# PEER layer on one core: signs of listed chunks tied to their chunk, dense part of U up to chunk 88, earlier use of the dense tiles for gathered U rows

## The chip, the cores and the metric

The kernel runs on one core of one Trainium2 chip. The metric is the device time of one execution in microseconds (us). The kernel before has a median of 1894.81 us in 3 runs (1887.17 to 1896.88). Engines are named as in the profile: PE (TensorE), PEld (its weight load), ACT (ScalarE), DVE (VectorE), POOL (GpSimd), SP (SyncE, here only a queue that starts DMAs).

## The reference

One decoder layer over 256 tokens of width 2048: attention of two kinds, attention into a memory, then PEER, a retrieval of single-neuron experts, and a last rmsnorm. The change touches PEER alone:

```python
q = (xt @ w_pq).reshape(T, PEER_HEADS, 2, PEER_D_KEY // 2)
s = jnp.einsum('thpd,hpkd->thpk', q, sub_keys)
top_s, top_i = lax.top_k(s, K)
...
best_s, best_c = lax.top_k(cand.reshape(T, PEER_HEADS, K * K), K)
expert = ia * PEER_N_KEYS + ib
gate = jax.nn.softmax(best_s, axis=-1)
...
a = jnp.einsum('td,ted->te', xb, u_tab[eb])
hidden = gb.astype(xb.dtype) * jax.nn.gelu(a)
return jnp.einsum('te,ted->td', hidden, v_tab[eb])
```

Each of 256 tokens picks 8 times 16 of 16384 experts. An expert has a row of U (2048 numbers) and a row of V.

## The kernel before

**Dense and listed chunks.** The 16384 experts are 128 chunks of 128. For chunks 0 to `C1` - 1 (83) the kernel multiplies U with all 256 tokens, whether an expert was picked or not (`u_chunk`, the "dense" chunks). For the rest, the "listed" chunks, it first finds which experts were picked by any token, writes the rows of their gates as packed lists to memory, and gathers only the U rows on these lists (`listed_products`). Experts are sorted by class: picked by one token only (`UONE`), by several tokens of one half of the sequence (`UFEW0`, `UFEW1`), or by both halves (`UALL`). `CAPS[2]` gives each class its number of tiles of 128 rows. Rows beyond a class go to `UALL`, and if that overflows as well, a slow loop (`rest`) does the remainder at the end.

**One dense chunk.** It has two halves. In each, SP loads half of the chunk's U (512 KB) into one of four `raw` tiles, ACT rounds it to `hi` (L75), DVE subtracts to get `lo` (L77; `self.last_lo` is the latest of these), and PE does 8 matmuls with `hi` (L93) and 8 with `lo` (L95). Then ACT and DVE join the two sums (L128, L129), and ACT applies gelu (L824).

**The table of gates.** The gates are scattered into a table in memory with 256 indirect writes by POOL (`put_gate`, L1170), 16 as each of 16 top-k results is finished; the kernel asks for four beside each block of work. By the counters in the code, 38 dense chunks have been emitted when the last top-k piece is out, 60 writes are then left, and `end` is 38 + 15 = 53. At chunk `end + 9` = 62 it emits the reads of the table for the listed chunks (`table_read`, L811), straight into their tiles `hb`. From chunk 63 on it takes items from `marks`: first one sign and count for each pair of listed chunks (`signs`, ACT L833 and DVE L834), up to six items a chunk, and then the seven steps that turn counts into positions (`lists`, ending in `where`, L1047). After these come 44 indirect writes (L1054) that place the listed rows, four a chunk. From chunk 65 to 82 one read a chunk fetches the gates of four dense chunks into a `raw` tile (L811, `gates`), and DVE multiplies them into the hidden values (L759).

**The listed part.** Each of 39 tiles reads its rows of gates (`lb`, L880), gathers 128 rows of U (`urows`, POOL L884), and, for class `UONE`, the matching tokens too (`xr`, POOL L895). `UONE` tiles are one DVE product (L904). The others are transposed by PE (L920), split by ACT and DVE (L921, L922) and multiplied (L93 and L95, or L937 and L940 where one half of the tokens is enough). Beside each quarter of a tile the kernel pops one step or one write of the lists of part 0 (chunks 0 to 75, 76 writes, L1054). `where` of these writes is ready at L1047 too.

**Tiles.** The dense chunks and the listed ones live in tiles of 8 chunks, 8 of them in pool `ba` (chunks 0 to 63) and 8 in pool `bb` (64 to 127). The same tiles are used again: `lb`, `urows` and `xr` of the first 14 listed tiles take theirs from `bb`, whose listed chunks are free once their rows are written; from the 15th on `urows` and `xr` come from `ba`, where a tile is free when the eight writes of part 0 that read it are done.

**Order.** Every engine works through its own queue in order. That order is not the order of the code: the framework sorts the instructions by priority along a timeline of its own (`schedule_with_timeline_sim=True`), so that an instruction whose inputs it holds to be ready can be put ahead of others that come earlier in the code. `add_manual_dep` adds a dependency that it must keep. After the listed part comes the V phase (L1249), which gathers V rows for all lists and ends with the norm and the stores.

Of the kernel before, what the change touches and what calls it, by code (L numbers as in the profile page):

```python
# [22 lines left out]
SYNC = mybir.DependencyInfo(mybir.DependencyClass.Sync, mybir.DependencyReason.DATA)  # L23
AF = mybir.ActivationFunctionType
# [15 lines left out]

C1 = 84
PARTS = ((0, 76), (76, 123), (C1, 128))
ONE0, ONE1, FEW0, FEW1, ALL = range(5)
CAPS = ((14, 14, 5, 5, 14), (10, 10, 4, 4, 10), (12, 4, 5, 18))
UONE, UFEW0, UFEW1, UALL = range(4)
UTILES = sum(CAPS[2])
assert PARTS[1][1] == C1 + UTILES
BASE, ROWS = [], []  # L50
for caps in CAPS:
    BASE.append([sum(caps[:j]) * 128 for j in range(len(caps))])
# [4 lines left out]
class Layer:  # L57
# [138 lines left out]
    def run(self):  # L196
        nc, tc, a = self.nc, self.tc, self.a
        with ExitStack() as top:
# [19 lines left out]
            self.rows = [self.dram.tile([n + (hi - lo) * 128, W], F32, name="rows%d" % part)  # L218
                         for part, (n, (lo, hi)) in enumerate(zip(ROWS, PARTS))]

# [423 lines left out]
    def peer(self):  # L644
        nc, tc, a = self.nc, self.tc, self.a
        with ExitStack() as es:
# [11 lines left out]
            def some(n):  # L658
                for _ in range(n):
                    if puts:  # L660
                        puts.pop(0)()

            with ExitStack() as e2:
# [55 lines left out]
                src = self.gw.tile([128, T], F32, tag="a", name="before_f", bufs=2)[:, :128]  # L719
# [4 lines left out]
                self.count = cl.tile([128, 2, 128], F32, name="count")  # L724
                self.rcount = self.count[:, :, C1:]
                self.over = cl.tile([128, 3], F32, name="over")
# [7 lines left out]
                marks, writes = [], []  # L734
                while c < C1:
                    if c % GROUP == 3 and first <= c + 5 < C1:
                        n = min(GROUP, C1 - c - 5)
                        self.table_read(self.buf[(c + 5) // GROUP][:, :n, :T], c + 5)
                    if c == end + 9:
                        for i in range(C1, 128, GROUP):  # L740
                            i -= i % GROUP
                            n = max(C1 - i, 0)
                            self.table_read(self.buf[i // GROUP][:, n:, :T], i + n)
                        for i in range(C1, 128, 2):
                            marks.append(lambda i=i: self.signs(self.buf[i // GROUP][:, i % GROUP:i % GROUP + 2, :T],
                                                                self.rcount[:, :, i - C1:i - C1 + 2]))
                        steps, writes = self.lists(2, ps, "sc", 2)
                        for p in range(0, len(steps), 2):
                            marks.append(lambda p=p: [f() for f in steps[p:p + 2]])
                    if c >= end + 12 and early:  # L750
                        g = early.pop(0)
                        t = self.st.tile([128, 4 * W], F32, tag="raw", name="gates", bufs=RAW)
                        t = t[:, :4 * T].rearrange("p (i t) -> p i t", t=T)
                        self.table_read(t, g)
                        done.setdefault(c + 1, []).append((g, t))
                    self.u_chunk(c, c >= first)
                    for g, t in done.pop(c, []):
                        d = self.buf[g // GROUP][:, g % GROUP:g % GROUP + 4, :T]
                        nc.vector.tensor_mul(d, d, t)  # L759
                        self.counts(g, g + 4)  # L760
                    some(4)
                    if c >= first and c % 4 == 3:
                        self.counts(c - 3, c + 1)
                    if c > end + 9:
                        if len(marks) > 4:
                            for _ in range(min(6, len(marks) - 4)):
                                marks.pop(0)()
                        elif marks:
                            marks.pop(0)()
                        else:  # L770
                            for _ in range(4):
                                if writes:
                                    writes.pop(0)()
                    c += 1
# [51 lines left out]
            nc.vector.tensor_mul(dst, dst, t)  # L826


    def signs(self, src, dst):

        n = src.shape[1]
        t = self.gw.tile([128, 2, T], BF16, tag="b", name="signs", bufs=2)[:, :n, :]
        self.nc.scalar.activation(t, src, AF.Sign)  # L833
        self.nc.vector.tensor_reduce(out=dst, in_=t.rearrange("p i (b t) -> p b i t", b=2),  # L834
                                     axis=AX.X, op=ALU.add, apply_absolute_value=True)

# [24 lines left out]
    def listed_products(self, beside):  # L861

        nc, ps, mm = self.nc, self.ps, self.nc.tensor.matmul
        v = nc.vector
        caps = CAPS[2]
        wide = sorted(((k + 0.5) / caps[c], c, k) for c in (UFEW0, UFEW1, UALL) for k in range(caps[c]))
# [8 lines left out]
        def start(n):  # L875
            cls, k = seq[n]
            if n % GROUP == 0:
                self.lbuf.append(self.bb.tile([128, GROUP, W], F32, tag="hb", name="lb", bufs=8))
            row = self.lbuf[n // GROUP][:, n % GROUP, :]
            ins = nc.sync.dma_start(row, self.listed(2, cls)[:, k, :])  # L880
            self.after(ins, 2)
            pool = self.bb if n < 14 else self.ba
            u = pool.tile([128, GROUP * W], F32, tag="hb", name="urows", bufs=8)[:, :D]
            nc.gpsimd.indirect_dma_start(  # L884
                out=u, out_offset=None, in_=self.a["Un"],
                in_offset=bass.IndirectOffsetOnAxis(ap=row[:, T:T + 1].bitcast(U32), axis=0),
                bounds_check=16383, oob_is_err=False)
            st = state[n] = {"row": row, "u": u, "cls": cls}
            if cls == UONE:
                best = self.gw.tile([128, 8], F32, tag="best", name="best", bufs=2)  # L890
                at = self.gw.tile([128, 8], U32, tag="at", name="at", bufs=2)
                v.max(out=best, in_=row[:, :T])
                v.max_index(out=at, in_max=best, in_values=row[:, :T])
                x = pool.tile([128, GROUP * W], F32, tag="hb", name="xr", bufs=8)[:, :D]
                nc.gpsimd.indirect_dma_start(  # L895
                    out=x, out_offset=None, in_=self.xrows,
                    in_offset=bass.IndirectOffsetOnAxis(ap=at[:, 0:1], axis=0),
                    bounds_check=T - 1, oob_is_err=False)
                st["x"] = x
# [60 lines left out]
        for n in range(ahead):  # L960
            start(n)
# [23 lines left out]
    def lists(self, part, pool, tag, bufs):  # L985


        nc, tc, cl = self.nc, self.tc, self.cl
        lo, hi = PARTS[part]
        n = hi - lo  # L990
        v = nc.vector
        cap, base = CAPS[part], BASE[part]
        sides = len(cap) - 1
# [185 lines left out]
    def plan(self):  # L1179

        self.seq, self.bundles, self.ends, self.sets, self.index = [], [], [], {}, {}
        self.homes = ([self.ba] * 8 + [self.bb] * 1) * 4 + ([self.ba] * 8 + [self.bb] * 8) * 4
        a, b = CAPS[:2]
        for lists in (((0, ONE0, 0, 5), (0, FEW0, 0, a[FEW0])),
# [16 lines left out]
    def after(self, ins, part):  # L1201
        assert len(self.written[part]) == PARTS[part][1] - PARTS[part][0]
        for w in self.written[part]:
            self.tc.add_manual_dep(ins.ins, w.ins.name, SYNC, reason="rows of the lists")

    def listed(self, part, cls):

        n, r = CAPS[part][cls], BASE[part][cls]
        return self.rows[part][r:r + n * 128, :].rearrange("(k p) w -> p k w", p=128)
# [197 lines left out]
    def rest(self, hidden_pair, products, out, kept):  # L1407
# [6 lines left out]
        with tc.If(count > 0):  # L1414
# [4 lines left out]
            def places(part):  # L1419
                lo, hi = PARTS[part]  # L1420
                n = hi - lo
                x = cl.tile([128, n], F32, tag="ok", name="rest_x")
                nc.vector.tensor_scalar(x, order[:, :n], self.over[:, part:part + 1], float(BIG),
                                        op0=ALU.is_ge, op1=ALU.mult)
                nc.vector.scalar_tensor_tensor(x, order[:, :n], float(ROWS[part]), x, op0=ALU.add, op1=ALU.add)
                at = cl.tile([128, n], U32, tag="where", name="rest_at")
                nc.vector.tensor_copy(at, x)
                return at
# [165 lines left out]
```

## Time and profile before

| what | value |
|---|---|
| median of 3 runs | 1894.81 us |
| the profiled execution's own time | 1893.41 us |
| its span, first to last instruction | 1891.6 us |
| mean granted PE clock in it | 0.936 |
| PE, PEld busy | 1624.2 us (86%), 1374.1 us (73%) |
| DVE, ACT, POOL busy | 1265.5 us (67%), 969.6 us (51%), 867.2 us (46%) |

A row of the windows view gives, for a stretch of the span, the busy time of PE, PEld, DVE, ACT and POOL with the number of their instructions, then the granted PE clock, the share of the DMA engines and GB/s. A row of the waits view names the waiting engine, tile and line, then what it waited for: us in total, times, the longest. A timeline row has the start, the length, the engine, the line and the operation, and in brackets the idle time before it and what ended it. The groups view has a line's instructions by shape: count, busy us, mean ns, and the idle time before them.

### The profile page before, as it was taken

To read this page: it belongs to the slowest core of one execution; us is meant where nothing else is said; L and a number is where in the kernel's file an instruction comes from. 1 tells how busy PE (TensorE), PEld (TensorE's weight loads), DVE (VectorE), ACT (ScalarE), POOL (GpSimd) and SP (SyncE) were. 2 spreads that over 40 slices of the span, in tenths; PEclk is the share of its full clock that TensorE was granted. 3 is DMA by queue.
4 is the path that set the end of the run, shared out by engine and by line. 5 is a ranking of instruction groups with operands and counts; after the bars stand their busy time and mean duration, and the time that the engine had idled before them with its cause. 6 is when DMAs were issued, how large, how long until landed. Compare 5 with 4: busy or idle time off the path is not lost. (4 is left out here: it accounts for less than half of the span.)

```text
span 1891.6 us, 25657 instructions
## 1 busy us (share of the span) xinstructions
PE 1624.2 (86%) x8790; PEld 1374.1 (73%) x8790; DVE 1265.5 (67%) x2345; ACT 969.6 (51%) x1490; POOL 867.2 (46%) x754
## 2 busy tenths in 40 slices
PE   8899999999998889999703999969448989899995
PEld 6788878878886778888603888758447877678874
DVE  6934664557688999999304559667335678677886
ACT  6434566655663446665204456444223447466765
POOL 5500001212256788888774000562777336886420
PEclk9999999999999989999956999989778999999997
DMA  7565345999655546666505667677377977998972
GB/s 273 185 229 185 127 163 171 397 391 361 194 173 188 169 130 191 200 190 190 136 1 202 210 190 265 219 261 272 124 249 292 383 298 290 373 412 321 414 313 68
DMA packets 140574, 444.38 MB, mean 235 GB/s; under 512 B 40112, under 2 KB 58230, under 8 KB 119952
## 3 DMA queue, kind: packets, MB, share of 16 engines
q1 hardware_dynamic: 91376, 217.68, 35.9%
q0 software_dynamic: 49056, 224.95, 31.0%
q8 instruction: 71, 1.16, 0.2%
q14 instruction: 71, 0.58, 0.1%
HBM read 384.12 MB, written 64.41 MB: 237 GB/s over the span
## 5 line engine op out<-in xcount | busy, mean ns | idle before, releaser
L93 PE MATMUL acc<-pair_f,hi 128*128 128x512 f32 x1872 | 496.5, 405 | 110.5 <-ACT hi L75 109.3
L77 DVE TENSOR_TENSOR lo<-raw,hi 128x1024 fp32r<-128x1024 f32 x346 | 432.2, 1253 | 206.8 <-ACT hi L75 179.7
L75 ACT ACTIVATE hi<-raw 128x1024 fp32r<-128x1024 f32 x350 | 368.4, 1057 | 317.7 <-PE acc L93 149.9
L93 PEld LDWEIGHTS acc<-pair_f,hi 128*128 128x128 f32 x1872 | 344.2, 195 | 173.3 <-ACT hi L75 111.9
L1170 POOL DMA_INDIRECT table<-total,place x256 | 327.0, 1277 | 94.7 <-issue 75.3
L95 PE MATMUL acc<-pair_f,lo 128*128 128x256 f32 x1872 | 277.3, 288 | 9.7 <-DVE lo L77 6.3
L95 PEld LDWEIGHTS acc<-pair_f,lo 128*128 128x128 f32 x1872 | 263.1, 194 | 30.7 <-DVE lo L77 8.1
L1054 POOL DMA_INDIRECT rows<-hb,where x128 | 139.6, 1091 | 48.7 <-issue 36.3
L1221 POOL DMA_INDIRECT vrows<-V,index x90 | 115.7, 1286 | 91.5 <-DVE lo L77 27.2
L86 DVE SCALAR_TENSOR_TENSOR lo<-vrows,val,hi 128x1024 fp32r<-128x1024 f32 x96 | 122.7, 1283 | 41.3 <-ACT hi L84 36.5
L84 ACT ACTIVATE hi<-vrows,val 128x1024 fp32r<-128x1024 f32 x96 | 109.1, 1147 | 70.0 <-PE out L1249 31.9
L93 PE MATMUL acc<-pair_x,hi 128*128 128x512 f32 x512 | 132.1, 396 | 0.0
L920 PE MATMUL ps_tp<-ident,urows 128*128 128x128 f32 x432 | 69.0, 295 | 63.4 <-DMA urows<-Un,lb 58.2
L77 DVE TENSOR_TENSOR lo<-vrows,hi 128x1024 fp32r<-128x1024 f32 x84 | 102.5, 1221 | 30.4 <-ACT hi L75 20.4
L834 DVE TENSOR_REDUCE count<-signs 128x4 f32<-128x512 bf16 x84 | 55.0, 677 | 100.1 <-ACT signs L833 99.2
L922 DVE TENSOR_TENSOR lo<-ps_tp,hi 128x512 fp32r<-128x512 f32 x108 | 72.7, 687 | 59.8 <-ACT hi L921 59.3
L921 ACT ACTIVATE hi<-ps_tp 128x512 fp32r<-128x512 f32 x108 | 63.3, 596 | 94.7 <-PE ps_tp L920 93.6
L920 PEld LDWEIGHTS ps_tp<-ident,urows 128*128 128x128 f32 x432 | 55.7, 152 | 71.7 <-issue 59.2
L75 ACT ACTIVATE hi<-vrows 128x1024 fp32r<-128x1024 f32 x84 | 88.2, 1053 | 36.8 <-PE out L1249 22.0
L93 PEld LDWEIGHTS acc<-pair_x,hi 128*128 128x128 f32 x512 | 91.4, 189 | 17.1 <-issue 1.4
L1249 PE MATMUL out<-hi,hh 128*128 128x512 f32 x264 | 84.3, 412 | 16.2 <-ACT hh L1256 8.1
L833 ACT ACTIVATE signs<-hb 128x512 bf16<-128x512 f32 x64 | 37.7, 622 | 111.9 <-DMA hb<-table 92.6
(423 smaller groups left out, 2820.8 us busy)
## 6 DMA issues: line engine op xcount, KB each, us to landing
raw<-U SPq DMA_DIRECT2D x168, 512.0 KB, 4.2
raw<-w_sb SPq DMA_DIRECT2D x32, 512.0 KB, 5.2
table<-zero POOLq DMA_DIRECT2D x16, 1024.0 KB, 10.7
raw<-w_out SPq DMA_DIRECT2D x32, 512.0 KB, 6.7
raw<-w_pq SPq DMA_DIRECT2D x32, 512.0 KB, 3.8
rows<-zero POOLq DMA_DIRECT2D x17, 903.0 KB, 7.2
listed<-rows SPq DMA_DIRECT2D x90, 129.0 KB, 8.5
gates<-table POOLq DMA_DIRECT2D x18, 512.0 KB, 3.8
```

The source lines that it names most:

```text
L75: nc.scalar.activation(hi, raw, AF.Copy)
L77: self.last_lo = (eng or nc.vector).tensor_tensor(out=lo, in0=raw, in1=hi.bitcast(F32), op=ALU.subtract)
L84: nc.scalar.activation(hi, raw, AF.Copy, scale=val)
L86: self.last_lo = nc.vector.scalar_tensor_tensor(lo, raw, val, hi.bitcast(F32), op0=ALU.mult, op1=ALU.subtract)
L93: mm(ps, hi[:, n * m:(n + 1) * m], pair[:, k, :], start=first and n == 0, stop=False)
L95: mm(ps[:, T:], lo[:, n * m:(n + 1) * m], pair[:, k, :T], start=False, stop=last and n == len(ks) - 1)
L920: nc.tensor.transpose(p[:, j * 128:(j + 1) * 128], st["u"][:, k * 128:(k + 1) * 128], self.ident)
L922: v.tensor_tensor(out=lo, in0=p, in1=hi.bitcast(F32), op=ALU.subtract)
L1054: ins = nc.gpsimd.indirect_dma_start(out=self.rows[part], out_offset=bass.IndirectOffsetOnAxis(ap=where[:, i - lo:i - lo + 1], axis=0), in ...
L1170: ins = self.nc.gpsimd.indirect_dma_start(out=self.table, out_offset=bass.IndirectOffsetOnAxis(ap=self.place[tb][:, s:s + 1], axis=0), in_ ...
L1221: nc.gpsimd.indirect_dma_start(out=raw, out_offset=None, in_=self.a["V"], in_offset=bass.IndirectOffsetOnAxis(ap=self.index[part, cls][:, ...
L1249: mm(out[tb][hf * 2 + q], h, v[:, q * 512:(q + 1) * 512], start=first and n == 0, stop=last and n == len(passes) - 1)
```

## The change

```diff
-C1 = 84
-PARTS = ((0, 76), (76, 123), (C1, 128))
+C1 = 88
+PARTS = ((0, 76), (76, 124), (C1, 128))
-CAPS = ((14, 14, 5, 5, 14), (10, 10, 4, 4, 10), (12, 4, 5, 18))
+CAPS = ((14, 14, 5, 5, 14), (10, 10, 4, 4, 10), (11, 4, 4, 17))
...
                             marks.append(lambda i=i: self.signs(self.buf[i // GROUP][:, i % GROUP:i % GROUP + 2, :T],
-                                                                self.rcount[:, :, i - C1:i - C1 + 2]))
+                                                                self.rcount[:, :, i - C1:i - C1 + 2], self.last_lo))
...
                         if len(marks) > 4:
-                            for _ in range(min(6, len(marks) - 4)):
+                            for _ in range(min(4, len(marks) - 4)):
                                 marks.pop(0)()
...
-    def signs(self, src, dst):
+    def signs(self, src, dst, behind=None):
...
-        self.nc.scalar.activation(t, src, AF.Sign)
+        ins = self.nc.scalar.activation(t, src, AF.Sign)
+        if behind is not None:
+            self.tc.add_manual_dep(ins.ins, behind.ins.name, SYNC, reason="not before its chunk")
...
-            pool = self.bb if n < 14 else self.ba
+            pool = self.bb if n < 11 else self.ba
```

Four things change. The sign of a pair of listed chunks now depends on the last `lo` of the dense chunk beside which it is emitted. Chunks 84 to 87 become dense, so there are 40 listed chunks and 36 listed tiles (11 `UONE`, 4 and 4 `UFEW`, 17 `UALL`; one `UONE`, one `UFEW1` and one `UALL` less), 40 writes instead of 44, 20 signs instead of 22, and part 1 of the V lists covers 48 chunk rows instead of 47. At most four marks are taken a chunk instead of six. The U rows and tokens of listed tiles 11 to 13 come from `ba` instead of `bb`.

## The prediction

> **What bounds the kernel now.** The page's slices of PE show a hole at about half of the span, so I read the waits view from 934 to 1046 us first, then the timelines of ACT, POOL and PE there, then the windows by stage.
>
> ```profile
> ACT signs L833 <- DMA hb<-table: 92.6, 3, 89.8
> PE acc L93 <- ACT hi L75: 88.1, 3, 84.1
> ...
> 934.00:1018.00 84.00, 0.19 (x2) 0.00 (x0) 1.20 (x2) 1.86 (x3) 64.17 (x67) 0.52 0.06 16
> ...
> 1046.00:1120.00 74.00, 74.00 (x425) 65.13 (x424) 36.95 (x41) 35.72 (x53) 0.00 (x0) 1.00 0.61 190
> ...
> 1212.00:1286.00 74.00, 53.28 (x242) 44.36 (x241) 41.80 (x59) 29.26 (x47) 45.89 (x45) 0.84 0.74 252
> ...
> 1336.00:1452.00 116.00, 54.64 (x342) 50.09 (x341) 40.74 (x72) 25.49 (x52) 90.37 (x84) 0.76 0.64 218
> 1452.00:1556.00 104.00, 94.46 (x631) 84.50 (x630) 73.05 (x141) 49.48 (x102) 42.42 (x40) 0.96 0.92 344
> 1556.00:1874.00 318.00, 294.62 (x1242) 228.77 (x1242) 243.90 (x335) 200.86 (x221) 170.79 (x132) 0.96 0.83 325
> ```
>
> ```profile
> 925.91 0.40 ACT L824 ACTIVATE hb<-hb 128x256 f32<-128x256 f32 x1
> 1016.14 1.15 ACT L833 ACTIVATE signs<-hb 128x512 bf16<-128x512 f32 x2 [89.83 <-DMA hb<-table]
> ...
> 1009.33 0.98 POOL L1170 DMA_INDIRECT table<-total,place  x1 [0.30 <-issue]
> 1012.16 6.86 POOL L811 DMA_DIRECT2D hb<-table  x8 [1.85 <-DMA table<-total,place]
> ...
> 1018.29 3.78 PE L93 MATMUL acc<-pair_f,hi 128*128 128x512 f32 x8 [84.10 <-ACT hi L75]
> ...
> 1046.28 2.00 PE L93 MATMUL acc<-pair_f,hi 128*128 128x512 f32 x8
> ...
> 1063.04 2.00 PE L93 MATMUL acc<-pair_f,hi 128*128 128x512 f32 x8
> ...
> 1096.56 2.00 PE L93 MATMUL acc<-pair_f,hi 128*128 128x512 f32 x8
> ```
>
> The reader is to see a queue blocked at its head. ACT stands before the first sign of a listed chunk from 926 to 1016 us. That sign needs the table's reads, these need the last scatter write, and POOL issues that one at 1009. Behind the sign in ACT's queue stands the next `hi`, which needs nothing of the table; without it PE has no work from 934.2 (1018.29 - 84.10) to 1018.3. In the quiet stage a half of a dense chunk takes (1096.56 - 1063.04) / 12 = 2.79 us, a chunk 5.59 us, with PE busy all the time. After the hole come a weaker stage (1212 to 1286, PE 53 of 74 us), a poor one in the listed part (1336 to 1452, 55 of 116), and then PE at 91 and 93%. So PE bounds the kernel wherever it is fed, and an earlier start of the V phase is worth its full length.
>
> **Where the sign will stand.**
>
> ```profile
> L93 PE MATMUL acc<-pair_f,hi 128*128 128x512 f32 x640 | 172.1, 413 | 108.8 <-ACT hi L75 108.8
> ...
> L1170 POOL DMA_INDIRECT table<-total,place x24 | 27.9, 1163 | 7.3 <-issue 7.3
> ...
> L1170 POOL DMA_INDIRECT table<-total,place x60 | 58.8, 980 | 18.3 <-issue 18.3
> ```
>
> The first row is the groups view from 1017 to 1286: 640 matmuls are 80 halves, 40 of 84 chunks, so the hole is at chunk 44. The code emits the first sign beside chunk 63; it was put 19 chunks ahead. The new dependency forbids this: a sign needs the last `lo` of chunk 63 or later, and DVE makes that only when PE has come so far. PE reaches chunk 63 at 934.2 + 19 x 5.59 = 1040 us. The other two rows are the scatter writes from 900 to 934, beside dense work, and from 934 to 1011, in the hole: (27.9 + 7.3) / 24 = 1.47 us each, and 1.28 us. The 60 that are left take 60 x 1.47 = 88 us, to 1022 instead of 1010. The reads follow as before, 12 us later; ACT got its first sign 6 us after the last write ended, hence now at about 1028, and the last sign of these was at 1037, hence now 1049 or, with U's loads at full rate beside the reads, some 1055. Signs need one group of 8 chunks per dense chunk, from 1042 to 1064. The data is there some 10 us ahead at both ends. So the stop goes: from 934.2 to 1046.28 there were 112.1 us and seven halves (19.6 us): **-92.5 us**. What is late next is the write chain, below.
>
> The Trainium skill, SBUF — State Buffer, section "Who interferes with whom", speaks against this: a DVE instruction with two SBUF inputs and a GpSimd instruction that reads SBUF exclude each other, the later one waiting for the whole of the earlier. The subtraction for `lo` is such an instruction, and the writes would now all run beside it; what that would give is the fourth rival. The trace does not bear out a full wait for each write: 1.47 us beside dense work against 1.28 us alone.
>
> **What is added.** Four dense chunks: 4 x 5.59 = **+22.3 us**. Nothing hides them for certain.
>
> Four signs and counts a chunk, for five chunks. Before, 18 pairs were done at 1016 to 1038, in the hole's wake; now they share the queues with dense work.
>
> ```profile
> 1160.00:1180.00 20.00, 20.00 (x119) 17.17 (x117) 18.52 (x33) 12.87 (x20) 2.11 (x4) 1.00 0.76 258
> ...
> L834 DVE TENSOR_REDUCE count<-signs 128x4 f32<-128x512 bf16 x84 | 55.0, 677 | 100.1 <-ACT signs L833 99.2
> ...
> L833 ACT ACTIVATE signs<-hb x18: 613/626/632, 1016.1 to 1037.1; 128x512 bf16<-128x512 f32 x18
> ...
> L77 DVE TENSOR_TENSOR lo<-raw,hi 128x1024 fp32r<-128x1024 f32 x346 | 432.2, 1253 | 206.8 <-ACT hi L75 179.7
> ```
>
> A quiet chunk costs ACT 35.7 / 74 x 5.59 = 2.7 us, and four signs 4 x 0.626 = 2.5 more: it fits. DVE has 2.8 us a chunk there, and 5.2 (18.52 / 20 x 5.59) in the stage of early gates, from chunk 65 on. Four counts are 2.7 us: chunks 63 and 64 fit, 65 to 67 need 7.9 and run over by 2.3 each, 6.9 us at most; a part falls into gaps. I take **+6 us**, between 0 (as in 1160 to 1180, where PE lost nothing) and 10. The new wait itself is short: by the last row `lo` ends about 1.25 us after its `hi`, and the `hi` behind the sign is made a half ahead of PE.
>
> **The write chain.**
>
> ```profile
> L1054 POOL DMA_INDIRECT rows<-hb,where x44 | 47.8, 1086 | 15.8 <-issue 12.8 <-DVE where L1047 2.7 <-DMA rows<-hb,where 0.3
> ...
> 1198.83 1.03 POOL L1054 DMA_INDIRECT rows<-hb,where  x1 [2.70 <-DVE where L1047]
> ...
> 1260.85 1.20 POOL L1054 DMA_INDIRECT rows<-hb,where  x1 [0.30 <-issue]
> ...
> 1284.23 1.03 PE L920 MATMUL ps_tp<-ident,urows 128*128 128x128 f32 x8
> ```
>
> A write costs (47.8 + 12.8) / 44 = 1.38 us. The chain is 62 us of writes and the reads of gates among them, then 22 us until PE transposes the first listed tile. In those stages `gates` tiles, whose reads stand behind writes on POOL, hold `raw` tiles that U needs: this is the weak stage from 1212. The first write moves by -92.5 + 6, and by one chunk (5.6) since four marks a chunk push the steps back by one: 1118 us. 40 writes end 56.5 us later, at 1174, and a listed tile can start at 1197. The dense chunks end at 1286 - 92.5 + 22.3 + 6 = 1222 if the weak stage loses what it lost before. So the chain, which ended together with the dense work, is now covered by it by 25 us, and I cost the weak stage, the four writes less and the later steps at no change. If the cover were gone, it would cost what the chain lags; the other way, four chunks at full pace could fill that stage (first rival).
>
> **The listed part.**
>
> ```profile
> PE ps_tp L920 <- DMA urows<-Un,lb: 58.2, 4, 22.4
> ...
> 1375.44 2.79 PE L920 MATMUL ps_tp<-ident,urows 128*128 128x128 f32 x12 [8.38 <-DMA urows<-Un,lb]
> ...
> 1405.60 2.79 PE L920 MATMUL ps_tp<-ident,urows 128*128 128x128 f32 x12 [21.23 <-DMA urows<-Un,lb]
> ...
> 1371.99 1.00 POOL L884 DMA_INDIRECT urows<-Un,lb  x1 [0.30 <-issue]
> ...
> 1399.61 1.05 POOL L884 DMA_INDIRECT urows<-Un,lb  x1 [0.31 <-issue]
> ...
> 1387.16 2.29 DVE L904 CUSTOM_DVE_ANT_0 urows<-urows,xr 128x2048 f32<-128x2048 f32 x1 [1.92 <-DMA xr<-xrows,at]
> ```
>
> ```profile
> 1328.74 0.60 PE L920 MATMUL ps_tp<-ident,urows 128*128 128x128 f32 x4
> 1329.10 0.70 PE L93 MATMUL acc<-pair_f,hi 128*128 128x512 f32 x2
> ...
> 1330.55 1.09 PE L93 MATMUL acc<-pair_f,hi 128*128 128x512 f32 x4
> ...
> 1331.95 1.09 PE L93 MATMUL acc<-pair_f,hi 128*128 128x512 f32 x4
> ...
> 1365.06 0.68 PE L937 MATMUL acc<-pair_f,hi 128*128 128x256 f32 x4
> ...
> 1365.97 0.69 PE L937 MATMUL acc<-pair_f,hi 128*128 128x256 f32 x4
> ```
>
> One `UALL` tile less is 4 x 1.40 us of products and 4 x 0.36 of transposes, 7.0; one `UFEW1` tile 4 x 0.91 + 1.4 = 5.1: **-12.1 us**, since the tail from 1452 is PE's. The `UONE` tile has no PE work; DVE and POOL have room there.
>
> Moving tiles 11 to 13 to `ba`: PE waits for gathers four times. The 21.2 us end with a gather issued at 1399.6, 12 us after the product of a `UONE` tile, which frees `bb` tiles, began; a gather ahead of it had left at 1372. I read this as tile 13 waiting for a place in `bb`, and the 8.4 us as tile 11 doing so. In `ba` they need 8 to 24 of part 0's writes first, and one more place is eight writes, 8 x 1.38 = 11.0. So: 29.6 us saved less 11.0: **-18.6 us**. The ends are -36 (29.6 and a later wait of about 6, nothing lost) and +11 (one place late, nothing saved).
>
> Sum against the profiled execution: 1893.4 - 92.5 + 22.3 + 6.0 - 12.1 - 18.6 = **1798.5 us**. That execution is 1.4 us under the median of before, which I leave aside.
>
> **The rivals.** First: the four chunks hide under the weak stage, where PE was idle 74 - 53.3 = 20.7 us: 1798.5 - 22.3 = 1776. For it: writes and dense work run side by side. Against: the reads of gates still stand behind writes in POOL's queue, and the new chunks come after the last of them. 15%.
>
> Second: `ba` starves the gathers. Places there come at POOL's pace, and POOL is busy 90 of 116 us with part 0's writes. Then the 18.6 are not gained and one place is late: 1798.5 + 18.6 + 11.0 = 1828. 14%.
>
> Third, on the other side: the stop stays, at another instruction. Signs and products of the dense chunks' early gates also need the table and carry no new dependency; put ahead on ACT or DVE, one would block the same queue until the same reads. Then 1893.4 + 22.3 + 6 - 12.1 = 1910, slower; it decides from a remaining stop of some 76 us without the gain in `ba`. 4%. Against it:
>
> ```profile
> 1129.20 0.55 POOL L811 DMA_DIRECT2D gates<-table  x1 [110.18 <-DMA raw<-U]
> ```
>
> their reads take `raw` tiles in turn with U's loads, and the first of them came 111 us, 20 chunks, after the hole's end.
>
> Fourth: the scatter writes slow down beside dense work. If each waited for one subtraction (1.25 us) they would end at 934 + 60 x 2.53 = 1086, the sign would come at 1092 instead of 1042, and the time would be 50 us more, 1848. 3%. The row of 1.47 us speaks against it.
>
> That a class overflows its tiles and the slow loop runs: from the reference's inputs I count 1306, 481, 500 and 2089 experts in the listed chunks for 1408, 512, 512 and 2176 rows. Under 1%.
>
> **How the numbers follow.** The forecast has 58%, the named rivals 37%, and 5% is unnamed, at either side. The range takes in the first and second rival and the ends of the unknown terms together in part: 1765 to 1840. About 0.5% is what a measurement of this kernel can tell from no change. Faster by more: 94%; within: 2%; slower by more: 4%.
>
> **What would show it.** Right: no wait of ACT for `hb<-table` over some us, PE full through 934 to 1100, first listed sign near 1042, first write of rows near 1118, V phase from about 1460. Wrong: a long wait of ACT or DVE on the table; the first transposes before 1205 (first rival); waits for `urows` over 58 us (second); scatter writes over 2 us each (fourth).

## The result, and the profile after

| what | before | after |
|---|---|---|
| median | 1892.29 us, 4 runs (1887.17 to 1896.88) | 1823.18 us, 4 runs (1817.37 to 1825.71) |
| ratio, 95% interval | 1 | 0.963 [0.959, 0.967] |
| profiled execution, its span | 1893.41, 1891.6 us | 1817.37, 1815.3 us |
| last dense product (L826) | 1288.5 us | 1245.4 us |
| V phase begins | 1551.5 us | 1476.7 us |

The changed kernel is 3.7% faster; the forecast of 1798.5 us was 25 us too low, and the range held the time. The profiled execution of after is the fastest of its four. In the code after, lines behind `signs` have numbers higher by two (the scatter writes are L1172, row writes L1056, transposes L922, the V phase L1251). First the windows view of after, with the columns of the prediction's rows:

```profile
934.00:1018.00 84.00, 82.58 (x472) 72.41 (x471) 41.51 (x45) 39.22 (x59) 65.72 (x61) 1.00 0.67 188
1042.00:1061.00 19.00, 9.64 (x54) 8.09 (x52) 4.19 (x5) 3.83 (x6) 0.00 (x0) 0.86 0.81 289
1061.00:1140.00 79.00, 67.27 (x364) 58.12 (x365) 74.19 (x120) 52.78 (x87) 7.96 (x15) 0.89 0.76 256
1140.00:1222.00 82.00, 64.75 (x330) 55.46 (x329) 48.47 (x71) 38.13 (x61) 51.70 (x47) 0.87 0.74 238
```

The first row is the old stop: PE had 0.19 of these 84 us and now has 82.58. The next two are new losses: 9.4 of 19 us, then 11.7 of 79 with DVE busy 74 of 79. Before, PE was busy for all of the 98 us from 1042 to 1140. The fourth is the weak stage, with 17 of 82 us lost. The timeline of after shows what happened at 1042, and then at 1124 to 1136:

```profile
1022.93 6.24 POOL L811 DMA_DIRECT2D hb<-table  x7 [4.35 <-DMA table<-total,place]
1040.37 0.56 POOL L811 DMA_DIRECT2D gates<-table  x1 [11.20 <-DVE lo L77]
1042.91 1.15 ACT L833 ACTIVATE signs<-hb 128x512 bf16<-128x512 f32 x2 [0.98 <-DVE lo L77]
1057.68 1.23 DVE L759 TENSOR_TENSOR hb<-hb,gates 128x1024 f32<-128x1024 f32 x1 [14.81 <-DMA gates<-table]
1060.01 1.22 DVE L77 TENSOR_TENSOR lo<-raw,hi 128x1024 fp32r<-128x1024 f32 x1
1061.28 1.01 PE L95 MATMUL acc<-pair_f,lo 128*128 128x256 f32 x3 [9.64 <-DVE lo L77]
...
1132.04 0.16 DVE L1037 TENSOR_TENSOR both<-both,f 128x40 bf16<-128x40 bf16 x1
...
1132.26 0.29 PE L1018 MATMUL ps_tot<-ones_b,both 128*40 128x128 bf16 x1 [7.85 <-DVE both L1037]
...
1136.50 3.78 PE L93 MATMUL acc<-pair_f,hi 128*128 128x512 f32 x8 [3.13 <-DVE ut L129]
```

The first listed sign comes at 1042.9, tied to its `lo` and not waiting for the table. But the first read of early gates (0.5 MB) is issued at 1040.4, while seven table reads of 1 MB and U's loads keep the DMA engines 94% busy (1023 to 1058, 337 GB/s). The product that needs it starts only at 1057.7. That product (L759) was put at the head of DVE's queue, so the next `lo`, which needs nothing of it, is late, and PE stops for 9.6 us. It is the old stop at about a tenth of its length, on DVE instead of ACT.

The loss from 1061 to 1140 is another one. PE stands 7.9 us at a matmul of the seven steps that turn counts into positions (L1018, which sums `both`), and 3.1 us soon after. The matmul needs a DVE step (L1037) that comes late in a DVE queue full of counts, products and subtractions. So here the blocked queue is PE's own. In the groups view of before the same matmul (L1016 there) ended no idle time:

```profile
L1016 PE MATMUL ps_tot<-ones_b,both 128*44 128x128 bf16 x1 | 0.2, 235 | 0.0
```

Two more views of after: a line's own instructions (count, min/median/max ns, first and last start), and one row of the waits.

```profile
L826 DVE TENSOR_TENSOR hb<-hb,ut x16: 411/418/427, 1136.9 to 1245.4; 128x256 f32<-128x256 f32 x16
...
L1251 PE MATMUL out<-hi,hh x264: 388/396/794, 1476.7 to 1796.4; 128*128 128x512 f32 x132
```

```profile
PE ps_tp L922 <- DMA urows<-Un,lb: 47.9, 5, 20.8
```

From the last dense product to the V phase 231.3 us pass; before it was 263.0. PE still waits 47.9 us for U rows in it, against 58.2.

### The profile page after: what moved, and what is told of

Its sections match the earlier page's. It is cut to its first block, busy times and chain, and to the rows that moved or that the text cites. A ratio compares the mean times of both kernels' runs of the same rounds, so it can differ in the third digit from the quotient of the medians.

```text
span 1815.3 us, 25728 instructions
## 1 busy us (share of the span) xinstructions
PE 1627.4 (90%) x8822; PEld 1375.2 (76%) x8822; DVE 1263.9 (70%) x2341; ACT 972.7 (54%) x1491; POOL 880.3 (48%) x746
## 3 DMA queue, kind: packets, MB, share of 16 engines
q1 hardware_dynamic: 92096, 221.48, 38.5%
## 5 line engine op out<-in xcount | busy, mean ns | idle before, releaser
L77 DVE TENSOR_TENSOR lo<-raw,hi 128x1024 fp32r<-128x1024 f32 x354 | 441.4, 1251 | 209.7 <-ACT hi L75 181.5
L75 ACT ACTIVATE hi<-raw 128x1024 fp32r<-128x1024 f32 x358 | 376.7, 1057 | 317.9 <-PE acc L93 144.3
L93 PE MATMUL acc<-pair_f,hi 128*128 128x512 f32 x1920 | 506.2, 403 | 23.3 <-ACT hi L75 18.9
L93 PEld LDWEIGHTS acc<-pair_f,hi 128*128 128x128 f32 x1920 | 352.2, 194 | 87.0 <-ACT hi L75 20.6
L1172 POOL DMA_INDIRECT table<-total,place x256 | 334.9, 1308 | 92.4 <-issue 75.2
L1223 POOL DMA_INDIRECT vrows<-V,index x90 | 124.7, 1386 | 79.8 <-DVE lo L77 23.3
L1056 POOL DMA_INDIRECT rows<-hb,where x128 | 135.9, 1062 | 46.7 <-issue 36.0
L86 DVE SCALAR_TENSOR_TENSOR lo<-vrows,val,hi 128x1024 fp32r<-128x1024 f32 x96 | 122.5, 1281 | 45.4 <-ACT hi L84 38.5
L77 DVE TENSOR_TENSOR lo<-vrows,hi 128x1024 fp32r<-128x1024 f32 x84 | 102.4, 1221 | 20.7 <-ACT hi L75 14.5
L922 PE MATMUL ps_tp<-ident,urows 128*128 128x128 f32 x400 | 61.0, 288 | 50.1 <-DMA urows<-Un,lb 47.9
L1251 PE MATMUL out<-hi,hh 128*128 128x512 f32 x264 | 85.5, 420 | 15.2 <-ACT hh L1258 12.6
L924 DVE TENSOR_TENSOR lo<-ps_tp,hi 128x512 fp32r<-128x512 f32 x100 | 66.8, 686 | 41.4 <-ACT hi L923 39.1
L922 PEld LDWEIGHTS ps_tp<-ident,urows 128*128 128x128 f32 x400 | 50.1, 149 | 56.8 <-issue 48.4
L1251 PE MATMUL out<-hi,hl 128*128 128x512 f32 x264 | 85.3, 407 | 1.2 <-DVE hl L1260 0.6
L1251 PE MATMUL out<-lo,hh 128*128 128x512 f32 x264 | 79.7, 403 | 0.4 <-DVE lo L77 0.4
```

The source lines that it names most:

```text
L75: nc.scalar.activation(hi, raw, AF.Copy)
L77: self.last_lo = (eng or nc.vector).tensor_tensor(out=lo, in0=raw, in1=hi.bitcast(F32), op=ALU.subtract)
L86: self.last_lo = nc.vector.scalar_tensor_tensor(lo, raw, val, hi.bitcast(F32), op0=ALU.mult, op1=ALU.subtract)
L93: mm(ps, hi[:, n * m:(n + 1) * m], pair[:, k, :], start=first and n == 0, stop=False)
L922: nc.tensor.transpose(p[:, j * 128:(j + 1) * 128], st["u"][:, k * 128:(k + 1) * 128], self.ident)
L924: v.tensor_tensor(out=lo, in0=p, in1=hi.bitcast(F32), op=ALU.subtract)
```

## The experiments

**The parts one by one, first try.** Four kernels: before with the tie alone; after without the tie; after with `n < 14`; after with a tie on the product of early gates as well.

```diff
-                                                                self.rcount[:, :, i - C1:i - C1 + 2], self.last_lo))
+                                                                self.rcount[:, :, i - C1:i - C1 + 2]))
```

(no tie; the tie alone is the reverse of it, put into the kernel before together with the new argument of `signs`)

```diff
-                        nc.vector.tensor_mul(d, d, t)
+                        ins = nc.vector.tensor_mul(d, d, t)
+                        tc.add_manual_dep(ins.ins, self.last_lo.ins.name, SYNC, reason="not before its chunk")
```

(tie on the product; for `n < 14` only that number changes)

> The kernel before with the tie of the listed signs alone (C1 stays 84, six marks, tiles from the 15th on in ba). Theory (the tie is nearly the whole gain; the new chunk boundary and the rest give little): no wait of ACT for the table over 5 us, a first listed sign near 1042 us, a new DVE wait on the first gates read of 10 to 20 us as in the changed kernel, and 1822 to 1845 us. Rival (the four dense chunks were needed to cover the write chain): PE stands idle over 20 us between its last dense matmul and the first listed transposes, and the time is over 1845 us.

> The changed kernel without the tie. Theory: the first listed sign is again put some 19 chunks ahead, ACT waits 85 to 95 us for the table, and the time is 1870 to 1900 us. Rival (fewer signs or four counts a chunk already keep the sign back): a wait under 40 us and under 1850 us.

> The changed kernel with U rows of listed tiles 11 to 13 back in bb. By the prediction's step (18.6 us from a place in ba instead of bb): 1836 to 1848 us, and waits of PE for urows some 19 us above the 47.9 us of the changed kernel. Rival (the place was not what held the gathers; the removed tiles gave the gain of that stage): within 8 us of the changed kernel.

> The changed kernel with the same kind of tie on the gates product of the dense chunks (L759): not before the last lo of the chunk beside which it is emitted. Theory (the part of the gain that is missing went to this product, at the head of DVE's queue for 14.8 us behind the table's reads): the DVE wait on the gates at 1042 us falls under 3 us, PE loses nothing up to 1060, and the time is 8 to 16 us under the changed kernel. Rival (DVE is full from 1061 to 1130 anyway, 66 of 69 us, so the stop only moves into that stage): within 4 us of the changed kernel.

They ran on another chip, on which the kernel before took 1943.88 us itself. Ratios to it: tie alone 0.993 [0.989, 0.998], no tie 0.999 [0.994, 1.004], `n < 14` 0.994 [0.985, 1.002], tie on the product 1.002 [0.998, 1.006]. So here no part did much. Three theories missed their times; the fourth was told against the kernel after, which was not run on this chip. The windows row of the tie alone shows why these times cannot stand beside the others:

```profile
760.00:840.00 80.00, 31.68 (x108) 22.60 (x107) 18.27 (x47) 12.53 (x19) 52.78 (x52) 0.59 0.20 60
```

PE, DVE and ACT were busy 32, 18 and 13 of 80 us in a stretch where the trace of before has PE busy for all 80 and DVE for 78. The first two of these waits of the kernel without the tie name no instruction that was waited for:

```profile
ACT hi L75 <- issue: 25.2, 9, 14.1
...
DVE lo L77 <- remote: 18.4, 1, 18.4
...
ACT signs L833 <- DMA hb<-table: 13.8, 1, 13.8
```

The last row is the useful one. Without the tie the sign waited for the table here too, but only 13.8 us, since dense work had fallen back behind POOL's scatter writes, which end the stop. This fits a simple account: where PE is late by another cause, a stop that POOL ends is shorter, and the tie is worth less. Why these engines stood still was not found.

**The parts again, on an undisturbed chip**, with a new try: the early gates read three dense chunks later.

```diff
-                    if c >= end + 12 and early:
+                    if c >= end + 15 and early:
```

> The kernel before with only the tie of the listed signs to their chunk; the set of listed U stays at chunk 84, six counts a chunk, n < 14. Before is 1892 us, after 1823 us on the chip where both were traced. The four kernels sent ahead of this one ran on a chip with long idle times of no shown cause in the dense part, so they are sent again in the hope of another chip; on the same kind of chip the ratios stay within 1% of 1. Theory (the tie is nearly the whole gain): 1820 to 1850 us, ratio to before 0.962 to 0.978. Rival (set from 88 and four counts a chunk are needed to cover the row writes): 1850 to 1875, ratio 0.978 to 0.99, with PE idle over 50 us between the end of the dense part and the first transposes.

> The kernel after with the tie alone taken away. Theory: the stop at the gates of chunk 44 is back, PE idle some 80 to 95 us ahead of the first listed sign, and the time is 1895 to 1925 us, ratio 1.00 to 1.02. Rival (the other three edits carry part of the gain): 1850 to 1885, ratio 0.98 to 0.995. If the dense part runs late by some other cause by d us, the stop is shorter by d, since POOL's puts end it.

> The kernel after, with the product of the early gates on the vector engine tied to the latest lo as well. Theory (that product stands ahead of lo and waits for the gates read for 15 us): the short stop at 1043 to 1060 us goes, PE gains 8 to 12 us there, time 1808 to 1816, ratio to before 0.955 to 0.960. Rival (the vector engine is full from 1061 to 1130 anyway, and what the stop gave is lost there): 1819 to 1828, ratio 0.961 to 0.966, the idle time only moved.

> The kernel after, with the reads of early gates beginning three dense chunks later (17 us), so that they start behind the seven table reads. Theory: the wait for the gates read at 1043 to 1058 goes, and the vector engine has room for counts first, so the table of places is done 5 to 15 us sooner: 1803 to 1815 us, ratio 0.953 to 0.959. Rival (the sum of the vector engine's work in chunks 66 to 84 decides): 1819 to 1828, ratio 0.961 to 0.966; the last gates come at chunk 86 and may cost up to 6 us more behind the dense part.

Before took 1889.36 us on this chip. Measured:

| kernel | us | ratio, 95% interval | last dense product | V phase begins | between |
|---|---|---|---|---|---|
| tie alone | 1824.77 | 0.967 [0.963, 0.970] | 1219.6 | 1485.7 | 266.1 |
| after without the tie | 1892.34 | 1.002 [1.000, 1.004] | 1316.1 | 1548.4 | 232.3 |
| after, product tied too | 1831.78 | 0.972 [0.969, 0.976] | 1255.4 | 1487.8 | 232.4 |
| after, gates later | 1815.5 | 0.963 [0.959, 0.967] | 1237.6 | 1471.6 | 234.0 |

*Tie alone and no tie.* The tie alone gives 0.967, all four edits 0.963, the other three alone 1.002. Within these intervals the tie carries the whole gain. The run without the tie came 2.7 us under its theory's 1895 to 1925, with a ratio as the theory had it. Without the tie the windows view has PE at 9.46 of the old 84 us again, and ACT's timeline the old head of the queue:

```profile
934.00:1018.00 84.00, 9.46 (x57) 8.25 (x55) 1.23 (x1) 1.06 (x1) 63.86 (x66) 0.57 0.09 23
```

```profile
1019.71 1.15 ACT L833 ACTIVATE signs<-hb 128x512 bf16<-128x512 f32 x2 [84.43 <-DMA hb<-table]
```

Rows of the tie alone, by line and by window:

```profile
L826 DVE TENSOR_TENSOR hb<-hb,ut x12: 414/418/426, 1140.2 to 1219.6; 128x256 f32<-128x256 f32 x12
...
L1251 PE MATMUL out<-hi,hh x264: 387/396/793, 1485.7 to 1805.7; 128*128 128x512 f32 x132
```

```profile
1042.00:1061.00 19.00, 8.02 (x45) 6.67 (x44) 2.11 (x3) 1.91 (x4) 0.00 (x0) 0.83 0.76 269
1061.00:1140.00 79.00, 64.63 (x357) 56.06 (x358) 74.06 (x111) 53.10 (x85) 6.88 (x13) 0.89 0.78 254
...
1220.00:1485.70 265.70, 193.97 (x1312) 176.80 (x1312) 146.68 (x284) 95.08 (x197) 147.25 (x141) 0.87 0.76 274
```

The short stop is here as well (PE busy 8 of 19 us), and so is the stand at L1018 (9.1 us). Both belong to the tie and not to the other edits.

*Product tied.* The theory named the stop rightly and was wrong about its worth. The windows and waits (from 1042 to 1222) of this kernel, in whose code the sign is L834, and then one wait of after in the same window:

```profile
1042.00:1061.00 19.00, 18.89 (x110) 16.52 (x109) 11.13 (x16) 10.69 (x18) 0.54 (x1) 1.00 0.93 342
1061.00:1140.00 79.00, 62.58 (x299) 52.45 (x300) 57.82 (x97) 40.35 (x67) 20.74 (x22) 0.87 0.55 176
1140.00:1222.00 82.00, 58.15 (x260) 49.02 (x259) 48.27 (x65) 32.43 (x50) 40.28 (x39) 0.81 0.78 265
```

```profile
ACT signs L834 <- DVE hb L759: 38.5, 12, 6.7
ACT hi L75 <- DMA raw<-U: 37.6, 27, 4.4
```

```profile
ACT hi L75 <- DMA raw<-U: 28.0, 18, 3.5
```

PE has 18.9 of 19 us at the place of the stop, and loses 16.4 and 23.9 in the next two, where after lost 11.7 and 17.3. The tied product comes later. Signs that need it wait at the head of ACT's queue (38.5 us), and `hi` waits for U 37.6 us, against 28.0 in after; that the `raw` tiles which hold the gates come free later would explain this, and was not tried apart. The stand at L1018 is gone, and PE now waits for `hi` alone. The interval lies above that of after: the wait was moved and grew. That is the rival's case, and worse than it.

*Gates later.* Its windows, and its timeline in the weak stage:

```profile
1042.00:1061.00 19.00, 19.00 (x111) 16.75 (x110) 16.02 (x22) 14.92 (x26) 0.56 (x1) 1.00 1.02 378
1061.00:1140.00 79.00, 76.09 (x435) 65.90 (x434) 72.27 (x118) 52.19 (x86) 20.74 (x23) 1.00 0.75 246
1140.00:1222.00 82.00, 48.91 (x221) 40.87 (x220) 42.67 (x59) 28.50 (x44) 40.67 (x39) 0.79 0.71 248
```

```profile
1120.91 1.02 POOL L1056 DMA_INDIRECT rows<-hb,where  x1 [0.89 <-DVE where L1049]
...
1161.18 0.98 POOL L1056 DMA_INDIRECT rows<-hb,where  x1 [0.30 <-DMA rows<-hb,where]
1162.14 0.61 POOL L811 DMA_DIRECT2D gates<-table  x1
...
1166.78 1.23 DVE L759 TENSOR_TENSOR hb<-hb,gates 128x1024 f32<-128x1024 f32 x1 [11.57 <-DMA gates<-table]
...
1168.04 1.15 ACT L833 ACTIVATE signs<-hb 128x512 bf16<-128x512 f32 x2 [14.11 <-DVE hb L759]
...
1169.10 1.04 ACT L75 ACTIVATE hi<-raw 128x1024 fp32r<-128x1024 f32 x1
...
1170.19 3.78 PE L93 MATMUL acc<-pair_f,hi 128*128 128x512 f32 x8 [12.30 <-ACT hi L75]
```

Here both new losses are nearly gone (0 of 19, 2.9 of 79), and the first row write is issued at 1120.9 instead of 1138.6, as the theory had it. But PE now loses 33 of 82 us in the weak stage. One read of gates, issued at 1162 behind 28 row writes in POOL's queue, holds the product, the sign, `hi` and PE in turn. From 1042 to 1222 PE loses 36.0 us in all, against 38.3 in after and 40.4 with the product tied. So what is gained at one point is given back at the next. The medians of 1815.5 and 1823.2 were each taken beside an own run of before (1889.36 and 1892.29), and the ratios, 0.963 and 0.963, cannot be told apart. By its ratio this run is the rival's.

**The gates in another queue.** If row writes in front of the gates' reads are the cause, the reads belong in SP's queue, where U's loads stand.

```diff
-    def table_read(self, dst, i):
+    def table_read(self, dst, i, queue=None):
...
-        ins = self.nc.gpsimd.dma_start(dst, self.by_key[:, i * T:(i + n) * T].rearrange("j (i t) -> j i t", t=T))
+        ins = (queue or self.nc.gpsimd).dma_start(dst, self.by_key[:, i * T:(i + n) * T].rearrange("j (i t) -> j i t", t=T))
...
-                        self.table_read(t, g)
+                        self.table_read(t, g, nc.sync)
```

> The kernel after, with the early gates read by the sync engine's queue, in which the U loads stand, and no longer by GpSimd's, in which the row writes stand; nothing else. Theory (in the weak stage the gates reads stand behind up to 28 row writes of 1.4 us, and the products, the counts, hi and PE wait for them: PE loses 38 us from 1042 to 1222): the loss between 1140 and 1222 falls from 17 to under 8 us, time 1800 to 1815, ratio to before 0.952 to 0.960. Rival (the chain from the table of places over the row writes to the first listed transposes sets the end, whatever PE does meanwhile): dense work ends earlier, and PE idles as long ahead of the first listed tile; 1818 to 1828, ratio 0.961 to 0.966.

> The same, and the reads begin three dense chunks later, as in the run with late gates alone (1815.5 us). Theory: both waits gone, PE loses under 20 of the 38 us from 1042 to 1222; time 1785 to 1805, ratio 0.945 to 0.955. Rival (row writes set the end): the first row write stays at about 1121, the first listed transposes at about 1203, and the time within 5 us of 1815, ratio 0.958 to 0.964.

> The kernel after, with n < 14 as before: listed tiles 11 to 13 take their U rows in the bb tiles again. Forecast of the prediction: this edit was worth 18.6 us, so 1842 us here, ratio 0.973. Theory from the trace of after (waits of the transposes for U rows only fell from 58 to 48 us): 8 to 12 us, 1831 to 1835, ratio 0.967 to 0.970. Rival (the gathers are late either way, as their indices or POOL's queue set them): 1820 to 1828, ratio 0.961 to 0.966.

These three fell on a chip with the same idle times, where before took 1961.73 us: 0.995 [0.992, 0.998], 0.998 [0.995, 1.001] and 0.988 [0.983, 0.993]. They settle nothing about the time on a quiet chip. Their traces give no clear sign for it either: from the first row write to the last dense product PE idled 13.5 and 19.4 us with the gates in SP's queue, and 19.2 us in the third kernel, which has them in POOL's. The idea stays open.

**`n < 14` once more**, on a quiet chip (before 1888.73 us):

> The kernel after with n < 14 as before, once more, since the first two runs of it fell on chips with long idle times of no shown cause. With the tie alone the dense part ended at 1220 us and the listed part took 266 us from there; after it ended at 1245 and took 231: 35 us less, in which one U tile and one FEW1 tile less were put at 12 by the prediction, and 18.6 at this edit. Theory (this edit carries what is left, some 20 us): 1840 to 1848 us, ratio to before 0.972 to 0.978, and the transposes wait 10 to 20 us longer for U rows than the 48 us of after. Rival (the shorter lists, and not this edit, made the listed part short; in the disturbed runs with n < 14 the transposes waited only 8 and 14 us for U rows): 1815 to 1828, ratio 0.959 to 0.966. On a disturbed chip again the ratio stays above 0.98 and tells nothing.

1825.93 us, ratio 0.967 [0.965, 0.969]. The same views as above, of this kernel:

```profile
L826 DVE TENSOR_TENSOR hb<-hb,ut x16: 414/418/427, 1133.4 to 1241.7; 128x256 f32<-128x256 f32 x16
...
L1251 PE MATMUL out<-hi,hh x264: 388/396/796, 1478.7 to 1804.0; 128*128 128x512 f32 x132
```

```profile
PE ps_tp L922 <- DMA urows<-Un,lb: 47.6, 5, 19.3
```

```profile
1242.00:1478.70 236.70, 177.57 (x1183) 160.25 (x1182) 131.06 (x255) 85.26 (x176) 142.72 (x132) 0.88 0.75 270
```

PE waits 47.6 us for U rows with the old places and 47.9 with the new: the edit changed nothing there. The rival holds: with four more dense chunks and 36 tiles the listed part is short by either choice (237.0 and 231.3 us), with 39 tiles it is long (263.0 in before, 266.1 with the tie alone). No run has the shorter lists without the four dense chunks, so what each of the two does to it is not separated. Whether the edit of the places is worth some us or none is within the intervals.

## Why the prediction was right, and where it was not

The direction and the main mechanism hold: a sign ahead of its time blocked ACT, and the tie undid it. The sum was off because three terms were mis-sized. Two of the errors cancel nearly: PE lost some 15 us more beside dense work than forecast, and the listed part fell by 17 us more. The third, a saving of 18.6 us that did not come, is most of what the time missed. That the miss stayed this small is in part luck. The start of the V phase, step by step, by the profiled executions of before, tie alone, after with `n < 14`, and after:

| step | forecast | measured |
|---|---|---|
| tie, with the signs and counts it brings beside dense work | -92.5 + 6.0 = -86.5 | 1551.5 to 1485.7: -65.8 |
| set from 88, shorter lists, four marks | +22.3 - 12.1 = +10.2 | to 1478.7: -7.0 |
| U rows of tiles 11 to 13 | -18.6 | to 1476.7: -2.0 |
| sum | -94.9 | -74.8 |

Each row compares single executions, and those of one kernel differ by some 8 us (1817.37 to 1825.71 for after). The last two measured values are no larger than that; by the ratios of the medians the three kernels stand at 0.967, 0.967 and 0.963.

**The stop, -92.5: right.** The sign stands at 1042.9 (forecast 1042), PE is full through the old hole, and the undone tie brings 84.4 us of waiting back. Scatter writes took (66.9 + 18.6) / 61 = 1.40 us each beside dense work, by the groups view from 934 to 1018:

```profile
L1172 POOL DMA_INDIRECT table<-total,place x61 | 66.9, 1097 | 18.6 <-issue 18.6
```

The fourth rival is out. The rule of the Trainium skill (SBUF — State Buffer, "Who interferes with whom") that spoke for it, a wait for the whole of a subtraction, is not borne out by this row.

**Signs and counts beside dense work, +6, at most 10: wrong.** PE lost 9.4 + 11.7 = 21 us from 1042 to 1140. The working counted DVE's load against the dense chunks alone and left out the order of the queues. Two things were missing. One is the product of early gates ahead of `lo` (9.6 us of PE). The other is the list steps' matmul in PE's queue, which waits for a step behind DVE's counts (7.9 us, and 3.1 after it). The third rival had the first of them ("put ahead on ACT or DVE, one would block the same queue"), but as 76 us or nothing; DVE's wait of 14.8 us on the table is the prediction's own sign of being wrong, in small. No rival had the second. The row against it, a first read 20 chunks after the hole, came from a trace in which the hole itself had kept the two bursts of reads apart. Without the hole that read starts 17 us after the first table read.

**Four dense chunks, +22.3: right at the end of the dense part.** The last dense product is 22.1 us later than with the tie alone (1219.6 to 1241.7) and, between the two kernels without the tie, 27.6 us (1288.5 to 1316.1). From 1140 to that product PE idles 20.9 us with the tie alone and 18.3 in after with `n < 14`, so the chunks did not fill the weak stage, which was the first rival's way. But the whole step, chunks and shorter lists, came out at -7.0, nearer to that rival's -12.1 than to the forecast's +10.2. From 934 us to the V phase PE's busy time rose by 13, about as forecast; its idle time fell by 20, and that was priced at nothing.

**The shorter lists, -12.1: too small.** From the tie alone to after with `n < 14` the listed part fell by 29.1 us, from 266.1 to 237.0. Some of this is bookkeeping: with four more dense chunks 23 transposes of listed tiles stand ahead of the last dense product, with the tie alone none. The working took PE's products of two tiles and left a `UONE` tile at nothing. But PE is not the bound there: it works 194 of 265.7 us and 178 of 236.7. Its work fell by 16 and its idle time by 13, and its waits for U rows fell from 66.3 us to 47.6. Every tile of any class is a gather, three fewer of 39. That the gathers set this pace fits these rows, and no run tried it.

**Tiles 11 to 13, -18.6: wrong.** The gather behind the 21 us wait was read as waiting for a place in `bb`. With places in `ba` the longest wait is 20.8 us, with those in `bb` 19.3. The trace of before shows what the gather stood behind. From 1373.3 to 1399.6 POOL issued 18 row writes of part 0 and one gather of tokens ahead of it, and never idled over 0.31 us between them:

```profile
1381.13 1.00 POOL L1054 DMA_INDIRECT rows<-hb,where  x1 [0.31 <-issue]
...
1398.32 0.98 POOL L1054 DMA_INDIRECT rows<-hb,where  x1 [0.30 <-issue]
1399.61 1.05 POOL L884 DMA_INDIRECT urows<-Un,lb  x1 [0.31 <-issue]
```

So when its turn came it waited for no place. In after POOL has no longer gap from 1274 to 1415 us. Why the order puts so many writes ahead of a gather, and what fewer would be worth, was not tried. The bounds of -36 and +11 held it, the value did not. The second rival (gathers starved in `ba`) is out: PE waits 47.9 us for U rows, and that rival's sign was over 58.

**The weak stage, "no change": right in sum, not for the reason given.** The first row write came at 1138.6 instead of 1118, as `where` waited behind a full DVE. Yet the run with gates later had it at 1120.9 and ended its dense part only 8 us sooner. PE's idle time from 1140 us to the last dense product is 20.8 us in after, against 20.7 in before's weak stage. By the trace of that run the end of the chain of writes was not what PE waited for, but the gates' reads among the writes; the runs that were to test this fell on the disturbed chip.

## What to carry to other kernels

In these traces an engine's queue stops at its first waiting instruction (84 us on ACT before; 14.8 on DVE and 7.9 on PE after), so a tie that holds one early reader of late data back calls for a look at every other reader of the same data, on every engine. Removing a stop also moves bursts of transfers together that the stop had kept apart: a row of the old trace that says "this comes long after" need not hold in the new one. When an instruction is late, look first at what its own queue issued just ahead of it: the late gather waited behind writes and not for its place. And where PE is idle a quarter of a stage, price a piece of work there by what the stage waits for and not by PE's part of it.

## What the runs showed of the hardware that was not expected

A read of 0.5 MB, issued 17 us after the start of seven reads of 1 MB from the same queue, with U's loads beside them (337 GB/s, DMA engines 94% busy), had its consumer start only 17.3 us later (1040.37 to 1057.68). In the run with gates later, one issued at 1162.14 was consumed at 1166.78, 4.6 us later.

On two of the chips the same program was 50 to 70 us slower (before 1943.88 and 1961.73 us, against 1889 to 1892), with idle times on PE, ACT and DVE, mostly in the dense part, that the trace gives no releaser for. POOL's scatter writes were held up far less: the last one began 8 us later than on a quiet chip with the tie alone (1018.6 to 1026.6) and the last dense product 79 us later (1219.6 to 1298.5). So on such a chip a stop that POOL ends is shorter, and the gain of removing it was smaller: the tie alone gave 0.993 there and 0.967 on a quiet chip.
